# Inverse roots of mean squares: one GpSimd power in place of an integer guess and Newton steps on VectorE

## The chip, the cores and the metric

The kernel runs on one core of a Trainium2 chip. The metric is the device time of one execution, in microseconds (us); the median of three runs is given. In the profile the engines are PE (TensorE's matmuls), PEld (its weight loads), DVE (VectorE), ACT (ScalarE), POOL (GpSimd) and SP (the queue that issues most transfers).

## The reference, cut to what matters

A denoising step of two layers over 17 tiles of 128 tokens (2048 latent tokens and a prompt of 128), width 1024. Layer 0 mixes gated linear attention (GLA) and an S5 state space model, layer 1 windowed attention and a short convolution. In four places rows are normalised by their root mean square:

```python
def rmsnorm(x, w):
    xf = x.astype(jnp.float32)
    y = xf * lax.rsqrt(jnp.mean(xf * xf, axis=-1, keepdims=True) + EPS) * w
    return y.astype(x.dtype)

h = rmsnorm(x, norm_w) * (1.0 + scale) + shift       # input of layer 0, input of layer 1: 1024 wide
o = rmsnorm(o, gla_onorm)                            # output of a GLA head: 128 wide
q, k = rmsnorm(q, q_norm_w), rmsnorm(k, k_norm_w)    # 8 query heads and 2 key heads: 64 wide
```

## The kernel before, in words

Each engine works through its own list of instructions in order, and semaphores tie the lists together. The program is written tile by tile; a scheduler then fixes the order of each list when the program is built, from its own estimates. So a change in one helper can move instructions that it does not touch.

The work runs in five stages. **Phase 1** (`phase1`, to about 275 us) walks the 17 tiles: the square sums of a tile's rows (L275, ACT), the inverse root (L276, for two tiles at a time), the scaling of the rows (L278, DVE), eight transposes on PE and the modulation on ACT (L236, L240), the split into a high and a low float32r part (L242, L244, DVE), and 24 products for each of three outputs (L337, L338, PE). The log-gates of two tiles follow (`gates`, L876 to L884). Beside it the scheduler puts the S5 parameters on DVE (`s5_setup`, L401 to L458); when these are ready, POOL computes the first S5 tables (L571 to L573, L655 to L657). The second stage is the **S5 core** with the first dense passes. The third, from about 700 us, holds the other dense passes, the backward GLA states and the modulation rows of layer 1. **Phase 4** (`phase4`, about 940 to 1390 us) takes one GLA chunk after another: POOL prepares decay arguments in eight steps (`gla_arg`, L976 to L979), ACT and DVE finish them (L980, L981), PE multiplies keys by queries (L1054), DVE merges the products (L1061), PE sums the values (L1069 to L1071), and then the chunk's rows are copied (L1073), squared (L1078), and scaled by the inverse root (L1079) on POOL (L1080). One chunk later the rows are transposed (L1152), and yet one later comes the out-projection (L100 to L102) with the residual (L1124), the square sum (L1166), the inverse root (L1168), the scaling (L1169) and the transposes (L236) for layer 1. The **layer 1** passes follow: queries, keys and gate (`qkv_pass`, about 1390 to 1640 us, with the inverse roots of ten heads a tile at L1234, their use at L1237 and L1238, rotary products on POOL at L1257 and transposes at L1269 and L1275), the convolution, and attention with the last projection (from 2015 us).

The helper that the diff touches is `rsqrt` (L83 to L95). It has four callers: L276 with 128x2 values (eight times, and once 128x1 for the last tile), L1079 with 128x4, L1168 with 128x1 and L1234 with 128x10 (17 times each): 60 calls.

Of the kernel before, what the change touches and what calls it, by code (L numbers as in the profile page):

```python
# [36 lines left out]
class Ring:  # L37
    """Slots taken in turn; each has a pool of its own, and is waited for by itself."""
# [10 lines left out]
class Kernel:  # L49
# [12 lines left out]
    def bank(self, tag, shape=(128, 512), dt=F32):  # L62
        """A PSUM bank: D dense products, T transposes, W the rest."""
        pool, bufs = (self.wp, 4) if tag == "W" else (self.pp, 2)
        return pool.tile(list(shape), dt, name="ps" + tag, tag=tag, bufs=bufs)

    def pair(self, shape):
        """Two PSUM banks, the first dimension over them."""
# [14 lines left out]
    def rsqrt(self, pool, tag, ss, shape, n):  # L83
        """1/sqrt(ss/n + eps) on VectorE."""
# [3 lines left out]
        t = pool.tile(shape, F32, name="rst", tag=tag + "t")  # L88
        nc.vector.tensor_scalar(v, ss, 1.0 / n, EPS, op0=OP.mult, op1=OP.add)
        nc.vector.tensor_scalar(y.bitcast(I32), v.bitcast(I32), -0.5, 1597463007.0, op0=OP.mult, op1=OP.add)  # L90
        for _ in range(3):
            nc.vector.scalar_tensor_tensor(t, y, -0.5, y, op0=OP.mult, op1=OP.mult)
            nc.vector.tensor_tensor(t, t, v, op=OP.mult)
            nc.vector.scalar_tensor_tensor(y, t, 1.5, y, op0=OP.add, op1=OP.mult)
        return y  # L95

    def mm3(self, out, lh, ll, rh, rl, start, stop):
        """out += (lh+ll)^T (rh+rl) without the product of the two low parts."""
        mm = self.nc.tensor.matmul
        mm(out, lh, rh, start=start, stop=False)  # L100
        mm(out, lh, rl, start=False, stop=False)  # L101
        mm(out, ll, rh, start=False, stop=stop)  # L102

    # ------------------------------------------------------------------ set-up
    def setup(self, es):
        nc, a = self.nc, self.a
        c = self.const = self.pool(es, "const", 1, side="left")
        self.ident = self.load(c, "ident", a["ident"])
        self.nw = self.load(c, "nw", a["nw"])
        cc = self.load(c, "cc", a["cc"])  # L110
        t = c.tile([128, 8, 2], F32, name="silt")
        # silu of the conditions, hi and lo
# [7 lines left out]
        # per layer: scale' = (1 + scale) norm_w and shift, feature-major; gate rows on all partitions  # L120
# [24 lines left out]
    def ada(self, l, j, wp, ring=None, room=None, bufs=4):  # L145
        """Columns 512 j.. of layer l's modulation rows: shift, scale' or the gate's rows."""
# [3 lines left out]
    def ada_cols(self, l, c0, n, wp, ring, room, bufs):  # L150
# [5 lines left out]
        # products of the rows' high parts, and of their low parts below  # L156
# [32 lines left out]
    def split_w(self, dst_h, dst_l, src, cols, stp, tag, ks):  # L189
        """dst_h/dst_l [128, 8, cols] of f32r from weight rows [1024, cols] in DRAM."""  # L190
# [7 lines left out]
    def ring(self, es, name, n, side):  # L198
        """Slots of 256 weight columns, hi and lo of f32r."""
        return Ring(*[self.pool(es, f"{name}{j}", 1, side=side) for j in range(n)])  # L200

    def slot(self, ring, src, nk=8, tag="w"):
        """256 weight columns [128 nk, 256] of DRAM -> [128, 2 (hi, lo), nk, 256] of f32r."""
# [12 lines left out]
    def stage(self, shape):  # L216
        """[128, ..] of the staging buffers."""
# [4 lines left out]
    def split(self, dst, src):  # L222
        """dst [128, 2 (hi, lo), ..] of f32r from src."""
# [3 lines left out]
    def make_h(self, l, s, xs, wk, hp=None):  # L227
        """h^T of one token tile from its normalised rows, [128, 8, 128]; with hp also its hi and lo of f32r."""
# [18 lines left out]
    # ------------------------------------------------------------------ phase 1  # L247
# [3 lines left out]
    def phase1(self, e5):  # L251
        nc, a = self.nc, self.a
        with ExitStack() as es:
# [34 lines left out]
            def tail(i):  # L288
                pl = self.bank("T", (96, 128))
                nc.tensor.transpose(pl, low.pop(i).rearrange("p z c -> p (z c)"), self.ident)  # L290
                # tile 0, then two tiles at a time
# [4 lines left out]
                # hi, hi, lo  # L296
# [6 lines left out]
            with ExitStack() as es2:  # L303
# [7 lines left out]
                # v | lf | lb, and u  # L311
                for k in range(8):
                    for c0, n, src in ((0, 544, 512), (544, 512, 1568)):
                        self.split_w(wh[:, :, c0 : c0 + n], wl[:, :, c0 : c0 + n], a["w_in_e"][:, src : src + n], n, ap, "w1st", (k,))
                    if k == 3:
# [4 lines left out]
                        # hi, lo, hi  # L320
# [38 lines left out]
    # ------------------------------------------------------------------ S5 parameters  # L359
    def s5_setup(self, es):  # L360
# [23 lines left out]
        with ExitStack() as e2:  # L384
# [27 lines left out]
            def exp(x):  # L412
                """e^x to float32's accuracy."""
# [13 lines left out]
                # below -87 the result is under float32's normal range: 0  # L427
# [9 lines left out]
            # th = k pi/2 + r  # L437
# [33 lines left out]
            # c = (lb - 1) / lam  # L471
# [15 lines left out]
            # [bb_re; bb_im] and [bb_im; bb_re]  # L487
# [10 lines left out]
            def powers(P, Q, hi):  # L498
                """P + iQ at 1 given: the powers up to hi, by doubling."""
# [22 lines left out]
            # e^{16 i theta}  # L522
# [6 lines left out]
            def unit(P, Q, u, v):  # L529
                """P + iQ back to modulus 1."""  # L530
# [18 lines left out]
    # ------------------------------------------------------------------ S5 core  # L549
    def s5_core(self, es):  # L550
# [7 lines left out]
        def weights(g):  # L558
            """C lambda^tau of a group; the kernel's rows when a quad's are there."""
# [40 lines left out]
        def tables(g0):  # L600
            """cos and [sin; -sin] of the chunk phases of two groups: [128, g, d, 138]."""
# [27 lines left out]
        def first(g):  # L629
            """Loads, phase tables, and lambda^tau bb for the chunks' end states."""  # L630
# [28 lines left out]
        def second(g):  # L659
            """The chunks' end states and the scan over chunks."""  # L660
# [9 lines left out]
            # the increments' weights, transposed: [128 (s, h), d, half, 128 (re|im)]  # L670
# [33 lines left out]
        def third(g):  # L704
            """Outputs (step, h) x chunk: latent chunks, one unused column, prompt chunks."""
# [33 lines left out]
    # ------------------------------------------------------------------ dense passes over h^T  # L739
    def fm_pass(self, hp, blocks, use, hd=None, tag="D", lag=0, parts=None):  # L740
        """Feature-major products: for pieces of 272 tokens and blocks of 128 columns, use(blk, piece, psum)."""
# [37 lines left out]
    def col_slots(self, ring, src, c0, n):  # L779
        """n columns from c0 as slots, and their blocks of 128."""  # L780
# [9 lines left out]
    def qz_pass(self, hp, blocks):  # L790
        """Queries and keys (four blocks) and the S5 gate (four blocks), feature-major."""
# [8 lines left out]
    def zg_pass(self, hp, blocks):  # L800
        """2 silu(z_gla), feature-major."""
# [10 lines left out]
    def glu_pass(self, p):  # L812
        """The S5 branch's gated linear unit and gate: ys_d."""
# [8 lines left out]
        # z of 128 features: [(g, h), step from the chunk's end, chunk]  # L822
# [949 lines left out]
```

## Time and profile before

| what | us |
|---|---|
| three runs | 2440.71, 2440.75, 2435.2 (median 2440.71) |
| span of the profiled execution, first to last instruction | 2431.9 |
| PE busy in that span | 2296.6 (94%) |
| DVE busy | 1770.2 (73%) |
| ACT, POOL busy | 1035.7 and 889.1 |

The page gives the profiled execution by its span and lists no time of its own beside it; the span is 3.3 us under the lowest run and 8.8 us (0.36%) under the median. An engine's busy time counts overlapping instructions once. [...]

### The profile page before, as it was taken

Reading aid. Unit: us, or ns where it says so; the run is one execution under the profiler, and the core shown is the slowest. Engines: PE = TensorE matmul, PEld = TensorE weight load, DVE = VectorE, ACT = ScalarE, POOL = GpSimd, SP = SyncE. Lnnn points to the kernel's source line nnn. Section 1 sums busy time; section 2 is a strip of 40 time slices with the busy share of each in tenths; the row PEclk is TensorE's granted clock in tenths of the full one; section 3 lists DMA queues with packets and bytes.
Section 4 is the critical chain, followed back from the end, with each engine's and each line's share of the span. In section 5 each row is a group of like instructions: output and inputs, shape, how many; then the busy total and the mean of one; then the engine's idle time right before and its main releaser. Section 6 shows DMA issues by size and latency. Waiting matters only on the chain.

```text
span 2431.9 us, 47923 instructions
## 1 busy us (share of the span) xinstructions
PE 2296.6 (94%) x17657; PEld 2118.7 (87%) x17657; DVE 1770.2 (73%) x4033; ACT 1035.7 (43%) x2462; POOL 889.1 (37%) x1351
## 2 busy tenths in 40 slices
PE   7998898899999997999999999999999998999998
PEld 4887787787788776888888999999999998999998
DVE  7998699999976887888888675556334336666765
ACT  7453532222244665455454432234112115565653
POOL 4117047777612525767675021111101102222221
PEclk8999999999999998899999999999999998999999
DMA  8442562233269776333333552235215213222221
GB/s 302 139 149 83 164 166 78 82 85 90 82 177 305 228 241 193 96 116 124 113 122 107 176 162 79 79 110 171 68 55 140 63 54 120 88 87 88 88 70 57
DMA packets 321906, 303.96 MB, mean 125 GB/s; under 512 B 44208, under 2 KB 281408, under 8 KB 321672
## 3 DMA queue, kind: packets, MB, share of 16 engines
q1 hardware_dynamic: 263672, 227.70, 31.3%
q10 hardware_dynamic: 48112, 42.38, 5.4%
q0 software_dynamic: 9888, 30.83, 3.4%
q8 instruction: 139, 2.28, 0.4%
q14 instruction: 95, 0.78, 0.1%
HBM read 212.43 MB, written 88.39 MB: 124 GB/s over the span
## 4 chain that ended last, share of the span: by engine, by line
PE 56%; DVE 6%; DMA 4%; issue 3%; ACT 2%; POOL 2%; SPq 0%; ACTq 0%; DVEq 0%; POOLq 0%
PE psW L102 7%; PE psW L100 7%; PE psW L101 7%; PE psD L100 7%; PE psD L102 6%; PE psD L101 6%; PE psP L1054 3%; PE psW L1483 2%; PE psW L1436 2%; PE psT L1471 2%; DMA wst<-in_w_ada_dram 1%; PE psP L1069 1%; PE psP L1071 1%; DMA zr<-z_d 1%; PE psT L928 1%
## 5 line engine op out<-in xcount | busy, mean ns | idle before, releaser
L100 PE MATMUL psD<-slot,yT 128*128 128x256 f32 x1088 | 316.3, 291 | 1.5 <-ACT yT L1098 1.3
L102 PE MATMUL psD<-slot,yT 128*128 128x256 f32 x1088 | 312.7, 290 | 0.0
L101 PE MATMUL psD<-slot,yT 128*128 128x256 f32 x1088 | 309.0, 285 | 0.0
L102 PE MATMUL psW<-hq,slot 128*128 128x272 f32 x1024 | 293.4, 288 | 0.0
L101 PE MATMUL psW<-hq,slot 128*128 128x272 f32 x1024 | 291.8, 286 | 0.0
L100 PE MATMUL psW<-hq,slot 128*128 128x272 f32 x1024 | 288.7, 287 | 0.0
L101 PE MATMUL psD<-hq,slot 128*128 128x272 f32 x768 | 225.6, 294 | 17.4 <-DVE hq L225 17.4
L100 PE MATMUL psD<-hq,slot 128*128 128x272 f32 x768 | 227.1, 298 | 11.0 <-ACT fo L787 10.5
L102 PE MATMUL psD<-hq,slot 128*128 128x272 f32 x768 | 225.3, 294 | 0.0
L100 PEld LDWEIGHTS psD<-slot,yT 128*128 128x128 f32 x1088 | 207.1, 190 | 9.0 <-ACT yT L1098 1.9
L101 PEld LDWEIGHTS psD<-slot,yT 128*128 128x128 f32 x1088 | 206.9, 190 | 2.2 <-issue 0.2
L102 PEld LDWEIGHTS psD<-slot,yT 128*128 128x128 f32 x1088 | 204.9, 190 | 4.4 <-issue 1.9
L102 PEld LDWEIGHTS psW<-hq,slot 128*128 128x128 f32 x1024 | 192.7, 188 | 0.0
L101 PEld LDWEIGHTS psW<-hq,slot 128*128 128x128 f32 x1024 | 192.1, 188 | 0.0
L100 PEld LDWEIGHTS psW<-hq,slot 128*128 128x128 f32 x1024 | 191.3, 189 | 0.0
L213 DVE TENSOR_TENSOR slot<-wst,slot 128x512 fp32r<-128x512 f32 x176 | 122.2, 705 | 65.7 <-ACT slot L212 65.1
L101 PEld LDWEIGHTS psD<-hq,slot 128*128 128x128 f32 x768 | 145.7, 190 | 25.7 <-DVE hq L225 21.0
L100 PEld LDWEIGHTS psD<-hq,slot 128*128 128x128 f32 x768 | 145.3, 190 | 19.1 <-ACT fo L787 12.9
L212 ACT CAST slot<-wst 128x512 fp32r<-128x512 f32 x176 | 106.6, 621 | 118.1 <-DMA wst<-in_w_in_o_dram 31.9
L1445 DVE CUSTOM_DVE_ANT_0 sc<-psW,amask,sink 128x512 f32<-128x512 f32 (+1 forms) x128 | 93.7, 732 | 83.5 <-PE psT L1471 76.5
L102 PEld LDWEIGHTS psD<-hq,slot 128*128 128x128 f32 x768 | 145.5, 190 | 7.9 <-issue 7.8
L980 ACT ACTIVATE arg<-arg 128x512 f32<-128x512 f32 x119 | 75.0, 630 | 141.5 <-POOL arg L979 132.1
(387 smaller groups left out, 6794.0 us busy)
## 6 DMA issues: line engine op xcount, KB each, us to landing
wst<-h_d SPq DMA_DIRECT2D x136, 272.0 KB
wst<-in_w_ada_dram SPq DMA_DIRECT2D x64, 256.0 KB
h_d<-hf SPq DMA_DIRECT2D x17, 512.0 KB
x_d<-x ACTq DMA_DIRECT2D x17, 512.0 KB
h_d<-hf ACTq DMA_DIRECT2D x17, 512.0 KB
wst<-h_d SPq DMA_DIRECT2D x34, 256.0 KB
qf<-qa_d SPq DMA_DIRECT2D x34, 256.0 KB
hq<-x_d SPq DMA_DIRECT2D x17, 512.0 KB
```

Source lines behind the costliest of these rows:

```text
L100: mm(out, lh, rh, start=start, stop=False)
L101: mm(out, lh, rl, start=False, stop=False)
L102: mm(out, ll, rh, start=False, stop=stop)
L212: nc.scalar.copy(r32(w[:, 0, k : k + 2]), st)
L213: nc.vector.tensor_tensor(r32(w[:, 1, k : k + 2]), st, w[:, 0, k : k + 2], op=OP.subtract)
L928: nc.tensor.matmul(kv[o : o + 64, pr, :], kt[:, pr, o : o + 64], v[:, h * 128 : h * 128 + 128], start=True, stop=True, tile_position=(0, o),)
L980: nc.scalar.activation(arg, arg, AF.Exp, scale=0.0625)
L1054: nc.tensor.matmul(pv[:, hh, pr, :], ak[o : o + 64, pr, :], aq[o : o + 64, pr, :], start=True, stop=True)
L1436: nc.tensor.matmul(out, r32(qs[:, j, h]), kk, start=j == 0, stop=j == 1)
L1445: V.tensor_tensor_reduce(sv, ps, mask, 1.0, sk[:, h : h + 1], op0=OP.add, op1=OP.max, accum_out=m)
L1471: nc.tensor.transpose(pt[:, c, :], t[:, 128 * c : 128 * c + 128], self.ident)
L1483: nc.tensor.matmul(po[kv][:, j % 2], r32(VV[:, b, kv]), r32(t[:, x, :, c, :]), start=c + x == 0, stop=c + x == nb)
```

## The change

`rsqrt` keeps the first step on DVE, v = ss/n + eps. The integer guess and the nine Newton operations on DVE go; one GpSimd `tensor_tensor` raises v to a column of -0.5 that is written once in `setup`. The rest of the diff takes out comments and docstrings, so line numbers after the helper are two lower.

```diff
     def rsqrt(self, pool, tag, ss, shape, n):
         nc = self.nc
         v = pool.tile(shape, F32, name="rsv", tag=tag + "v")
         y = pool.tile(shape, F32, name="rsy", tag=tag + "y")
-        t = pool.tile(shape, F32, name="rst", tag=tag + "t")
         nc.vector.tensor_scalar(v, ss, 1.0 / n, EPS, op0=OP.mult, op1=OP.add)
-        nc.vector.tensor_scalar(y.bitcast(I32), v.bitcast(I32), -0.5, 1597463007.0, op0=OP.mult, op1=OP.add)
-        for _ in range(3):
-            nc.vector.scalar_tensor_tensor(t, y, -0.5, y, op0=OP.mult, op1=OP.mult)
-            nc.vector.tensor_tensor(t, t, v, op=OP.mult)
-            nc.vector.scalar_tensor_tensor(y, t, 1.5, y, op0=OP.add, op1=OP.mult)
+        e = self.mhalf if len(shape) == 2 else self.mhalf.unsqueeze(2)
+        nc.gpsimd.tensor_tensor(y, v, e.to_broadcast(shape), op=OP.pow)
         return y
...
         self.ident = self.load(c, "ident", a["ident"])
+        self.mhalf = c.tile([128, 1], F32, name="mhalf")
+        nc.gpsimd.memset(self.mhalf, -0.5)
```

The scheduler's new order shows at three places. First, DVE in phase 1, at the last tile's inverse root (s5A and wu are tables of the S5 parameters; now two lines lower). Before:

```order
L89 TENSOR_SCALAR rsv<-ss_124 128x1
L278 TENSOR_SCALAR xt<-xt,rsy 128x1024 x2
L405 TENSOR_TENSOR s5A_1970<-s5A_1970,wu_2256 128x576
L405 TENSOR_TENSOR s5A_1971<-s5A_1971,wu_2256 128x576
L343 COPY vo<-psW 128x272
L90 TENSOR_SCALAR rsy<-rsv 128x1
L299 TENSOR_TENSOR lr<-psT,lr 32x128
```

Now:

```order
L403 TENSOR_TENSOR s5A_1902<-s5A_1902,wu_2188 128x576
L403 TENSOR_TENSOR s5A_1903<-s5A_1903,wu_2188 128x576
L240 CAST ht<-hf 128x512
L242 TENSOR_TENSOR ht<-hf,ht 128x1024
L88 TENSOR_SCALAR rsv<-ss_126 128x1
L341 COPY vo<-psW 128x272
L297 TENSOR_TENSOR lr<-psT,lr 32x128
L240 CAST ht<-hf 128x512
L874 TENSOR_TENSOR gm<-b_124,psW 128x512 x2
L276 TENSOR_SCALAR xt<-xt,rsy 128x1024
```

The last tile's inverse root now comes after the S5 tables, and five other instructions stand between its first step (now L88) and the scaling that uses it (now L276).

Second, POOL at the same time: the first S5 tables (ct and e; L571 to L573 and L655 to L657 before, two lower now) with the last tile's power among them. Now:

```order
L882 DMA b_d<-ge 128x4x256
L569 TENSOR_TENSOR ct_2742<-s5M,s5CY 128x272
L570 TENSOR_TENSOR ct<-s5R,s5CX 128x272
L569 TENSOR_TENSOR ct_2747<-s5M,s5CY 128x272
L570 TENSOR_TENSOR ct<-s5R,s5CX 128x272 x9
L654 TENSOR_TENSOR e<-s5R,s5X 128x256 x2
L570 TENSOR_TENSOR ct<-s5R,s5CX 128x272
L571 TENSOR_TENSOR ct<-ct,ct_2742 128x272
L570 TENSOR_TENSOR ct<-s5R,s5CX 128x272
L90 TENSOR_TENSOR rsy<-rsv,mhalf 128x1
L571 TENSOR_TENSOR ct<-ct,ct_2747 128x272
```

The power (L90) stands behind 17 of these tables in POOL's list; before, POOL had no part in an inverse root.

Third, POOL in a chunk of phase 4, where q is the last decay argument of a chunk. Now:

```order
L966 TENSOR_TENSOR q<-qk 128x256
L90 TENSOR_TENSOR rsy<-rsv,mhalf 128x1
L974 TENSOR_TENSOR arg<-B 128x2x64
L975 TENSOR_TENSOR arg<-B 128x2x64
L976 TENSOR_TENSOR arg<-B 128x2x64
L977 TENSOR_TENSOR arg<-B 128x2x64
L90 TENSOR_TENSOR rsy<-rsv,mhalf 128x4
L974 TENSOR_TENSOR arg<-B 128x4x32
L1078 TENSOR_TENSOR gy<-gy,rsy 128x512
```

Each chunk has gained the two powers here, and the scaling of the rows (gy, L1080 before) has moved up among the decay arguments, from behind the third group to the middle of the second.

## Rows read from the trace of the kernel before

**Rows 1.** The page: span, and busy time of each engine.

```profile
span 2431.9 us, 47923 instructions
PE 2296.6 (94%) x17657; PEld 2118.7 (87%) x17657; DVE 1770.2 (73%) x4033; ACT 1035.7 (43%) x2462; POOL 889.1 (37%) x1351
```

**Rows 2.** Windows: stretch, length, busy per engine (instructions), PE clock, DMA share, GB/s.

```profile
60.00:180.00 120.00, 116.38 (x748) 105.24 (x746) 115.94 (x382) 62.86 (x136) 15.76 (x30) 1.00 0.45 146
...
220.00:240.00 20.00, 13.15 (x65) 10.84 (x64) 16.20 (x16) 7.21 (x14) 9.58 (x13) 0.83 0.17 60
...
970.00:980.00 10.00, 6.19 (x34) 5.16 (x34) 9.57 (x19) 3.13 (x5) 10.00 (x19) 0.50 0.18 52
...
1050.00:1200.00 150.00, 148.97 (x1229) 129.41 (x1228) 129.71 (x307) 76.68 (x190) 107.33 (x195) 1.00 0.38 120
...
1500.00:1635.00 135.00, 135.00 (x1131) 135.00 (x1130) 73.93 (x190) 32.88 (x76) 25.21 (x45) 1.00 0.30 88
```

**Rows 3.** Groups by line: two of four removed DVE operations; busy us, mean ns, idle.

```profile
L93 DVE TENSOR_TENSOR rst<-rst,rsv 128x1 f32<-128x1 f32 (+3 forms) x180 | 39.7, 221 | 3.8
...
L90 DVE TENSOR_SCALAR rsy<-rsv 128x1 int32<-128x1 int32 (+3 forms) x60 | 11.1, 185 | 0.8
```

**Rows 4.** Timeline of DVE: start, us, instruction; a chain of nine by itself (first, last).

```profile
61.68 0.16 DVE L92 SCALAR_TENSOR_TENSOR rst<-rsy 128x2 f32<-128x2 f32 x1
...
63.25 0.16 DVE L94 SCALAR_TENSOR_TENSOR rsy<-rst,rsy 128x2 f32<-128x2 f32 x1
```

**Rows 5.** Timeline of DVE: a removed operation between others.

```profile
21.92 0.15 DVE L93 TENSOR_TENSOR rst<-rst,rsv 128x2 f32<-128x2 f32 x1
21.99 0.69 DVE L167 TENSOR_TENSOR w1l<-wada,w1l 128x512 fp32r<-128x512 f32 x1
```

**Rows 6.** Timeline of DVE: the last tile's chain of nine (first, last), beside POOL's tables.

```profile
184.76 0.60 DVE L92 SCALAR_TENSOR_TENSOR rst<-rsy 128x1 f32<-128x1 f32 x1
...
189.66 0.57 DVE L94 SCALAR_TENSOR_TENSOR rsy<-rst,rsy 128x1 f32<-128x1 f32 x1
```

**Rows 7.** Timeline of PE, 60 to 240 us: five of eight waits, with what ended each.

```profile
100.68 0.73 PE L338 MATMUL psD<-w1h,ht 128*128 128x512 f32 x2 [1.70 <-DVE ht L244]
...
180.10 0.73 PE L338 MATMUL psD<-w1h,ht 128*128 128x512 f32 x2 [1.08 <-DVE ht L244]
...
196.66 0.52 PE L337 MATMUL psW<-w1h,ht 128*128 128x272 f32 x2 [2.76 <-DVE ht L244]
...
225.27 0.39 PE L337 MATMUL psW<-w1h,ht 128*128 128x272 f32 x1 [3.69 <-DVE gm L876]
...
236.03 0.66 PE L236 MATMUL psT<-ident,xt 128*128 128x128 f32 x4 [1.71 <-DVE lr L299]
```

**Rows 8.** Timeline of DVE: a conversion beside POOL's tables.

```profile
210.29 14.21 DVE L242 CAST ht<-hf 128x512 fp32r<-128x512 f32 x1 [1.10 <-ACT hf L240]
```

**Rows 9.** Timeline of PE at the start of phase 4: first and last of three waits.

```profile
971.91 1.23 PE L1054 MATMUL psP<-arg 64*128 64x128 f32 x8 [0.65 <-DVE rsy L94]
...
978.40 0.79 PE L1069 MATMUL psP<-sf,hq 64*128 64x128 f32 x2 [2.21 <-DVE hq L1061]
```

**Rows 10.** Lines of POOL: a small copy and a small product (min/median/max ns).

```profile
L1311 POOL COPY crow<-crow x28: 184/184/246, 1638.2 to 1984.3; 128x2 f32<-128x2 f32 x28
...
L1257 POOL TENSOR_TENSOR au<-an,ropes x64: 516/528/1017, 1409.0 to 1616.4; 128x160 f32<-128x160 f32 x64
```

**Rows 11.** Groups by line: POOL's longest computing instruction.

```profile
L1422 POOL TENSOR_TENSOR qs<-qf,qs 128x1024 fp32r<-128x1024 f32 x17 | 40.6, 2391 | 101.6 <-DVE pT L225 60.5 <-ACT qs L1421 41.1
```

**Rows 12.** Timeline of POOL: first of the S5 tables, and one near their end.

```profile
183.29 0.65 POOL L571 TENSOR_TENSOR ct<-s5M,s5CY 128x272 f32<-128x272 f32 x1 [4.32 <-DVE s5A L405]
...
222.97 1.24 POOL L571 TENSOR_TENSOR ct<-s5M,s5CY 128x272 f32<-128x272 f32 x2
```

**Rows 13.** Timelines of DVE and PE in the query pass: a tile's rows ready, their transposes.

```profile
1460.80 0.28 DVE L1266 TENSOR_TENSOR ao<-an,au 128x128 f32<-128x128 f32 x1
...
1465.42 0.60 PE L1269 MATMUL psT<-ident,ao 128*128 128x128 f32 x4
```

## The prediction

> **What bounds the kernel now.** I read the page first: PE is busy for 2296.6 of 2431.9 us [rows 1], so at most 135 us of the span can be won by anything that makes PE wait less, and an engine with spare time can lose work without the end moving. The windows say where those 135 us are [rows 2]. From 1050 us on, through phase 4 and the query pass, PE is busy for 148.97 of 150 and 135.00 of 135 us at a granted clock of 1.00: there the matmuls are the bound, DVE has a seventh to nearly half of its time free, and a faster inverse root moves nothing. In phase 1 the picture differs: from 60 to 180 us DVE is busy for 115.94 of 120 us and PE for 116.38, so the two run head to head. The timeline of PE then gives the reasons of its stops: eight waits between 60 and 240 us [rows 7], every one ended by DVE. Three of them, from 100.68 to 180.10, come to 3.7 us; five, from 196.66 to 236.03, to 9.6 us. At the start of phase 4 there are three more, from 971.91 to 978.40, of 3.8 us together, the first of which names the Newton steps [rows 9]. These 17 us are what the change can reach. The S5 core holds no inverse root, and PE's list is word for word the same there in both programs.
>
> **What is removed.** 60 calls lose ten DVE operations each: the guess 60 times and three kinds of Newton operation 180 times each, 600 in all, at a mean of 185 to 221 ns [rows 3], so about 120 us of busy time. What DVE gains is less: an operation between others takes 0.07 us until the next one starts [rows 5], while a chain by itself costs about 0.2 for each, 1.73 us for nine [rows 4] and 1.9 with the guess. Over the first seven calls of phase 1 that follow 45 us that is 70 operations, between 5 and 14 us. The last call is dearer: its nine operations run from 184.76 to 190.23, 5.5 us, while POOL computes [rows 6]. So DVE gets back between 10 and 19 us of the first 190; I take 15, ten of them before the last call. Of the other 51 calls, 34 lie in phase 4 and 17 in the query pass, where PE covers them; if PE were faster there, they would be worth 51 times up to 1.9 us.
>
> **What is added.** 60 powers on POOL, and a memset that nothing waits for. The trace has no power. From below its price is that of POOL's smallest two-column copy, 0.184 us; from above, with nothing better, POOL's longest computing instruction, 2.39 us for 128x1024 [rows 10, 11]. I take 0.5 us, near the 0.528 of a product with a broadcast operand over 160 columns [rows 10], which is the nearest shape in kind; both ends stay in the range. At 0.5 us an inverse root lasts less than the 1.73 us chain even with two hand-overs between engines, which I put at 0.2 us each from the spacing of dependent DVE operations in the same chain. At 2.39 it lasts about a microsecond longer, but DVE is free meanwhile, except where the scaling stands right behind v, as in the second to fourth call.
>
> [...]
>
> **What is moved: phase 1 (minus 6.5 us).** With 15 us less on DVE, the split parts of a tile (L242, L244) come earlier, and the three waits of 3.7 us before the tables go. The wait of 2.76 at 196.66 follows directly on the dear chain and should go as well. That is 6.5 us. The four later waits, 6.9 us, have another cause: a conversion took 14.21 us from 210.29 [rows 8], to the end of a row of POOL tables that runs from 183.29 to about 224.2 [rows 12]. The tables stay, so I leave these 6.9 us and the lowered clock there (0.83 from 220 to 240) as they are. New is a wait: the last tile's power stands behind 17 tables on POOL, about 12 us at some 0.7 each, and DVE's scaling of that tile's rows waits for it, with the next split parts queued behind. Because the S5 parameters are finished 5 to 14 us sooner, by the DVE time won before them, DVE has that much in hand, so I charge nothing; without that cover it costs up to 5 us.
>
> [...]
>
> **Phase 4's start (minus 1.2 us).** From 965 to 979 us the second chunk has no other matmuls beside it, PE runs at a clock of 0.50, and DVE and POOL are both full (9.57 and 10.00 of 10 us from 970 to 980) [rows 2]. DVE loses ten operations there, 0.7 to 1.9 us by the bounds above, and PE's waits of 3.8 us [rows 9] are what that could shorten. But POOL gets a power, and the scaling of the rows moves up before decay arguments that used to come first. I take minus 1.2, between minus 3.8 and plus 3. Later in phase 4 and in the query pass: nothing, covered by PE. In the query pass a tile's rows are ready at 1461.1 and transposed at 1465.42 [rows 13], 4.3 us of slack on top of the 1.9 us chain that goes.
>
> Sum: 6.5 + 1.2 = 7.7 us off the profiled span of 2431.9, that is 2424.2. The median of the runs stands 8.8 above that span; with the same distance, 2433.0.
>
> **The rivals.**
> - *Hidden anyway.* The scheduler's new list puts other S5 steps where the Newton steps were, so the split parts come no earlier and PE keeps its waits; phase 4's start gives and takes. For it: DVE is full either way from 60 to 180 us. Against: S5 work is finite, and 15 us less must show. The time is 2437 to 2444.
> - *The blocked conversion goes too.* The tables then meet other DVE work, so the 6.9 us vanish, with up to 3 us of clock, and all of phase 4's 3.8: 3.7 + 2.8 + 6.9 + 3 + 3.8, about 20 off, 2420.
> - *A longer block.* The tables start up to 14 us sooner and hold another conversion for some 14 us as in [rows 8], or DVE stands for the last tile's power. PE has split parts in hand, so it loses some 8 to 14 us, with up to 3 at phase 4's start; the 6.5 won before go against it: 2442 to 2451.
> - *A slow power makes the query pass wait (slower).* If the power is evaluated column by column in software, ten columns cost far more than 0.5 us. The point from which it decides is 4.3 + 1.9 = 6.2 us for a 128x10 power: beyond it the transposes of every tile come late on PE's list. At 10 us each of 17 tiles loses 3.8, some 65 us: about 2500. Against: POOL's longest row is 2.39 us for 1024 columns. For: nothing in the trace bounds a power.
>
> **How the numbers follow.** About 0.3% (7 us) is what a measurement of this kernel can tell from no change, so the line runs at 2433.4. The forecast (4 to 13 us off) has 0.50, two thirds of it beyond the line; hidden 0.22; the conversion gone too 0.12; a longer block 0.08, of which 0.05 is slower; a slow power 0.08. Faster: 0.34 + 0.12 = 0.46. Same: 0.16 + 0.22 + 0.03 = 0.41. Slower: 0.13. The range leaves out the slow power and a few hundredths at each end: 2420 to 2450.
>
> **What would show it.** Right: no PE wait ended by L244 between 60 and 200 us, DVE busy about 15 us less up to 190, a POOL row for L90 of about half a microsecond, phase 4 and the query pass as long as before. Wrong: a L90 row of several microseconds; a DVE wait at the last tile's scaling that names POOL's power and is followed by a PE wait; PE gaps in the query pass before the transposes; or phase 1 as long as before with DVE less full.

## The result, and the profile after

The changed kernel takes **2452.07 us** (median of 4 runs, 2449.5 to 2452.27); the kernel before, run beside it, 2439.45 (4 runs, 2435.2 to 2440.75). The ratio is 1.0055, 95% interval 1.0039 to 1.0070: slower by 12.6 us, 2 us above the upper end of the predicted range. The profiled execution is one of 2452.01 us; that of before was one of 2435.2 us, 4 us under its median.

The page of the changed kernel, span and busy times [rows 1]:

```profile
span 2450.2 us, 47334 instructions
PE 2302.0 (94%) x17657; PEld 2124.8 (87%) x17657; DVE 1669.6 (68%) x3433; ACT 1037.3 (42%) x2462; POOL 942.3 (38%) x1412
```

DVE did lose 100.6 us of work. PE is no less busy, but the span is 18.3 us longer. The windows (busy of PE, PEld, DVE, ACT, POOL, then PE's clock) tell where [rows 2]:

```profile
60.00:180.00 120.00, 116.66 (x752) 105.56 (x751) 111.20 (x321) 60.65 (x129) 18.96 (x34) 1.00 0.42 136
200.00:220.00 20.00, 14.44 (x77) 12.54 (x77) 16.18 (x13) 8.84 (x20) 12.49 (x18) 0.83 0.24 79
220.00:240.00 20.00, 8.97 (x39) 7.64 (x40) 13.91 (x8) 1.96 (x7) 9.42 (x16) 0.66 0.08 27
...
1050.00:1200.00 150.00, 149.90 (x1248) 130.38 (x1246) 107.16 (x186) 77.34 (x190) 107.78 (x199) 1.00 0.39 120
1500.00:1635.00 135.00, 135.00 (x1133) 135.00 (x1132) 59.87 (x100) 30.01 (x71) 44.51 (x54) 1.00 0.27 82
```

Phase 4 and the query pass are full, as before. Between 200 and 240 us PE stands for 16.6 of 40 us. The granted clock falls in each of the two long stops: in slices of 5 us it is 0.62 and 0.69 from 200 to 210 us (in slices of 1 us, 0.50 from 202 to 208), 1.00 from 210 to 220, then 0.67, and 0.50 from 225 to 235. PE's timeline gives the waits of phase 1 [rows 7]:

```profile
48.31 1.12 PE L234 MATMUL psT<-ident,xt 128*128 128x128 f32 x4 [3.85 <-ACT hf L238]
...
104.68 0.74 PE L336 MATMUL psD<-w1h,ht 128*128 128x512 f32 x2 [1.54 <-DVE ht L242]
...
120.15 0.52 PE L335 MATMUL psW<-w1h,ht 128*128 128x272 f32 x2 [1.65 <-DVE ht L242]
...
203.88 0.82 PE L335 MATMUL psW<-w1h,ht 128*128 128x272 f32 x2 [6.18 <-DVE ht L242]
...
231.03 1.22 PE L336 MATMUL psD<-w1h,ht 128*128 128x512 f32 x2 [11.49 <-DVE ht L242]
```

DVE at the same place (idle time before an instruction in brackets), beside the conversion of [rows 8]:

```profile
189.07 1.28 DVE L874 TENSOR_TENSOR gm<-b,psW 128x512 f32<-128x512 f32 x2 [2.91 <-PE psW L873]
194.00 7.09 DVE L276 TENSOR_SCALAR xt<-xt,rsy 128x1024 f32<-128x1024 f32 x1 [3.65 <-POOL rsy L90]
...
202.15 0.41 DVE L240 CAST ht<-hf 128x512 fp32r<-128x512 f32 x1
202.60 1.23 DVE L242 TENSOR_TENSOR ht<-hf,ht 128x1024 fp32r<-128x1024 f32 x1
...
210.85 0.43 DVE L240 CAST ht<-hf 128x512 fp32r<-128x512 f32 x1
213.11 16.60 DVE L240 CAST ht<-hf 128x512 fp32r<-128x512 f32 x1 [1.83 <-ACT hf L238]
```

and POOL, whose power stands where the order showed it, behind 17 tables:

```profile
181.71 0.75 POOL L569 TENSOR_TENSOR ct<-s5M,s5CY 128x272 f32<-128x272 f32 x1 [0.66 <-DVE s5A L403]
...
193.40 0.57 POOL L90 TENSOR_TENSOR rsy<-rsv,mhalf 128x1 f32<-128x1 f32 x1
193.95 0.77 POOL L571 TENSOR_TENSOR ct<-ct,ct 128x272 f32<-128x272 f32 x1
...
199.91 0.64 POOL L569 TENSOR_TENSOR ct<-s5M,s5CY 128x272 f32<-128x272 f32 x1
206.03 1.04 POOL L345 COPY l<-vo 128x96 f32<-128x96 f32 x1 [5.49 <-ACT vo L342]
```

Two words for what follows. DVE **stands** when it is idle for a result, here 3.65 us for the last tile's power. It is **held** when its own row is long while POOL computes: the scaling, 0.75 us in the median of its calls, lasts 7.09, until just after POOL's run of tables ends at 200.55 (199.91 + 0.64), and a conversion of 0.43 lasts 16.60.

The table gives, for the same PE instruction in two traces, how much later it starts than in the profile of before (from the traces of the experiments below too; e13 is the kernel before with a tile that nothing reads, so it serves as a second profile of before):

| start in before, us | after | e13 | e1 | e2 | e3 | e5 | e9 | e14 |
|---|---|---|---|---|---|---|---|---|
| 45.30, first L337, first product of phase 1 | +5.2 | -0.6 | +0.6 | +5.0 | +4.4 | +4.7 | +5.6 | +4.4 |
| 282.69, last L337, end of phase 1 | +13.9 | -0.8 | +0.4 | +13.3 | -0.4 | +2.8 | +2.5 | -8.4 |
| 940.34, first L1054 of phase 4 | +14.9 | +4.2 | +4.2 | +20.2 | +3.2 | +6.3 | +4.0 | -3.4 |
| 1342.99, last L1054 | +16.3 | +0.7 | -0.2 | +23.7 | +3.7 | +8.2 | +6.4 | -2.0 |
| 1654.70, first L1363, after the query pass | +16.5 | +1.1 | +0.6 | +23.8 | +3.0 | +6.9 | +5.0 | -2.5 |
| 2427.26, last product | +18.3 | +0.7 | +2.4 | +27.3 | +2.4 | +8.9 | +5.1 | -0.6 |

So of the 18.3 us between the two profiles 13.9 exist when phase 1 ends. Later rows differ by up to 4.2 us even between before and e13, so a difference of that size in one profile is not read as an effect. Where an expectation below gives the start of the first product (56 us, or 60 to 61), it counts from a point 10.6 us earlier than the profile does: that is the row at 45.30 here.

### The profile page after: what moved, and what is told of

Same layout as the page of the kernel before. It is cut to its first block, busy times and chain, and to the rows that moved or that the text cites. A ratio compares the mean times of both kernels' runs of the same rounds, so it can differ in the third digit from the quotient of the medians.

```text
span 2450.2 us, 47334 instructions
## 1 busy us (share of the span) xinstructions
PE 2302.0 (94%) x17657; PEld 2124.8 (87%) x17657; DVE 1669.6 (68%) x3433; ACT 1037.3 (42%) x2462; POOL 942.3 (38%) x1412
## 4 chain that ended last, share of the span: by engine, by line
PE 55%; DVE 4%; issue 4%; DMA 4%; POOL 3%; ACT 2%; SPq 0%; ACTq 0%; DVEq 0%; POOLq 0%
PE psW L96 7%; PE psW L97 7%; PE psW L98 7%; PE psD L96 6%; PE psD L97 6%; PE psD L98 6%; PE psW L1481 2%; PE psW L1434 2%; PE psP L1052 2%; PE psT L1469 2%; PE psP L1067 1%; PE psP L1069 1%; DMA zr<-z_d 1%; POOL arg L974 1%; POOL arg L976 1%
## 5 line engine op out<-in xcount | busy, mean ns | idle before, releaser
L90 POOL TENSOR_TENSOR rsy<-rsv,mhalf 128x1 f32<-128x1 f32 (+3 forms) x60 | 72.4, 1207 | 309.1 <-DVE rsv L88 278.7
```

What stands on the lines that cost most here:

```text
L90: nc.gpsimd.tensor_tensor(y, v, e.to_broadcast(shape), op=OP.pow)
```

## The experiments

Line numbers of the variants are shifted by a few; the tiles' names tell which line it is. Times are medians, ratios are against the kernel before, run beside each. Theory A: the loss is made in phase 1. Theory B: the power itself is dear, wherever something waits for it.

**e1 and e2: the two halves of the change.** Newton kept in phase 1 (e1, the test as shown), or everywhere else (e2, with the test turned round).

```diff
+        if tag == "rs0":
+            nc.vector.tensor_scalar(y.bitcast(I32), v.bitcast(I32), -0.5, 1597463007.0, op0=OP.mult, op1=OP.add)
+            for _ in range(3):
...
+            return y
         nc.gpsimd.tensor_tensor(y, v, e.to_broadcast(shape), op=OP.pow)
```

> The three-step Newton form stays in phase 1 (its 9 calls); the other 51 roots go to the power. Every engine's order in phase 1 is then the one of the kernel before, and from phase 4 on about the changed kernel's. Theory A (the loss is made in phase 1: first products 4 to 5 us late, the block of S5 tables some 9 us longer): the time comes back to 2437 to 2442 us, the first product of phase 1 starts near 56 us and the DVE waits of PE in 180 to 260 us are again near 10 us. Theory B (the power itself costs, 1.07 us in the median where 0.5 was taken, on every call that something waits for, most of all the 128x10 calls of phase 4 and of the query pass): the time stays at 2448 to 2452 us.

> The reverse: the power in phase 1 only, Newton in phase 4 and the query pass. Every engine's order in phase 1 is the changed kernel's. Theory A: 2449 to 2454 us, first product near 61 us, two DVE waits of PE of about 6 and 11 us between 200 and 245 us. Theory B: 2437 to 2442 us.

e1: 2439.66 us, ratio 1.0003 (0.9992 to 1.0014). e2: 2459.02, 1.0074 (1.0055 to 1.0093). Theory B falls: 51 powers from phase 4 on cost nothing that shows, and nine in phase 1 bring the whole loss. e2 is even above the changed kernel; the table puts the difference after phase 1, where e2 has Newton and the changed kernel the power. As e1 and before do not differ there, I do not read a gain of the power from it; why the two parts do not add is open.

**e3: one call.** Newton for the last tile alone; the diff is against e1.

```diff
-        if tag == "rs0":
+        if tag == "rs0" and shape[1] == 1:
```

> The changed kernel with Newton for the last tile's row (128x1) alone, ten instructions on DVE at the place of the POOL power that stood behind 17 S5 tables; all else keeps its order but for a handful of rows. Theory A1 (in the block it is DVE's standing for that power, 3.65 us, and then the scaling held 7.09 us): PE's DVE waits in 180 to 260 us fall from 19 us to about 10 us and the time to 2441 to 2445 us. Theory A2 (the block is long because the S5 tables run packed together on POOL and hold whatever DVE runs, with or without this power): the waits stay at 15 us or more and the time at 2449 to 2453 us.

2439.84, ratio 0.9999 (0.9989 to 1.0010). One of 60 calls carries all of the loss, more than either theory of the expectation gave it. PE's DVE waits from 180 to 260 us fall from 18.9 to 4.4 us. The scaling is there at once, and the hold of a conversion is back in the form of [rows 8]:

```profile
187.62 0.79 DVE L284 TENSOR_SCALAR xt<-xt,rsy 128x1024 f32<-128x1024 f32 x1
...
212.96 12.25 DVE L248 CAST ht<-hf 128x512 fp32r<-128x512 f32 x1 [1.11 <-ACT hf L246]
```

The first product is still 4.4 us late, and by the end of phase 1 that is gone: the late start is absorbed in the block.

**e4: the late start.** In the changed kernel ScalarE squares tiles 2 and 3, after waiting 2.99 us for their load, before it scales tile 0; in the kernel before it scaled tile 0 first (at 42.50). After:

```profile
44.39 1.06 ACT L273 ACTIVATE sqj<-xt 128x1024 bf16<-128x1024 f32 x1 [2.99 <-DMA xt<-in_xs_dram]
...
46.77 2.88 ACT L238 ACTIVATE hf<-psT,msh,msc 128x128 f32<-128x128 f32 x8
```

```diff
...
-                    nc.scalar.activation(junk, xt[j], AF.Square, accum_out=ss[:, j : j + 1])
+                    with self.tc.issue_after(self.hf_first.ins) if i == 2 else ExitStack():
+                        nc.scalar.activation(junk, xt[j], AF.Square, accum_out=ss[:, j : j + 1])
```

> The changed kernel with ScalarE's squares of tiles 2 and 3 ordered behind tile 0's first eight scale-and-shift instructions, as they stood in the kernel before; the order of some other rows of phase 1 moves with it. If the 4 to 5 us at the first product come from ScalarE standing for the load of tiles 2 and 3 ahead of that work: first product back at 56 to 57 us, and 3 to 5 us less in all (2447 to 2449 us) if nothing else moves. If it comes from late weights or from the w1l subtractions on POOL: the first product stays at 60 to 61 us.

The first product is back (1.0 us late), and the median is 2447.32, ratio 1.0039 (1.0024 to 1.0055). So the cause of the late start is shown. What it is worth is not: the profiled run was one of 2455.35 us, and its block is the changed kernel's (a scaling of 7.70, a conversion of 16.60 us).

**e5: the last row called earlier.** It changes place with tiles 14 and 15, whose power now falls into the block.

```diff
-                if i % 2 and i + 1 < NTILE:
+                if i % 2 and i + 1 < NTILE - 1:
                     rows(i + 1)
...
                 if i == 10:
+                    rows(16)
                     self.s5_setup(e5)
```

> The changed kernel with the last tile's load, square, power and scaling called ahead of the S5 set-up, so that its power is issued on POOL before the tables (all else moves by a few rows; no Newton anywhere). Theory A1 (the loss is DVE standing at the last tile's scaling, for a power that is queued behind 17 tables, and then held in it while the tables run on): no scaling is left inside the block, one hold of 12 to 14 us at a conversion stays as before, PE's DVE waits in 180 to 260 us fall to about 10 us, and the time to 2437 to 2442 us. Rival (Newton's ten small instructions helped in another way, by breaking up the POOL tables while they ran beside them): the time stays above 2446 us, since no such instructions are here either.

2442.24, ratio 1.0013 (1.0003 to 1.0023). The rival falls, but the edit did less than meant: DVE stands 3.87 us for the other power, and then two scalings pass unheld:

```profile
194.71 1.78 DVE L276 TENSOR_SCALAR xt<-xt,rsy 128x1024 f32<-128x1024 f32 x2 [3.87 <-POOL rsy L90]
...
216.34 10.78 DVE L240 CAST ht<-hf 128x512 fp32r<-128x512 f32 x1 [1.11 <-ACT hf L238]
```

**e6, e7, e8: the form of the held instruction.** The last tile's scaling (e6), the conversions of tiles 11 to 16 as well (e7), and the same in the kernel before (e8), as operations of two tensors.

```diff
-                    nc.vector.tensor_scalar(xt[j], xt[j], rs[:, n : n + 1], None, op0=OP.mult)
+                    if j >= 16:
+                        nc.vector.tensor_tensor(xt[j], xt[j], rs[:, n : n + 1].to_broadcast([128, 1024]), op=OP.mult)
...
-                nc.vector.tensor_copy(r32(h[:, 0, kk * 4 : kk * 4 + 4]), f[:, kk * 4 : kk * 4 + 4])
+                d, g = r32(h[:, 0, kk * 4 : kk * 4 + 4]), f[:, kk * 4 : kk * 4 + 4]
+                if two:
+                    nc.vector.tensor_tensor(d, g, g, op=OP.max)
...
```

> The changed kernel with the last tile's scaling written as a product of two tensors (the row's factor read for each element) in place of a one-tensor instruction; the power stays behind the tables and DVE still stands for it. Tells the stand (3.65 us) from the hold (7.09 us) inside theory A1. If the hold is of one-tensor instructions with both ends in SBUF alone: the scaling takes 1.2 to 2.5 us and 5 to 6 us come back in the block, though the time falls by as much only if the next hold doesn't take the place (2444 to 2448 us). If any instruction is held at that place: 7 us again and 2450 to 2453 us.

> As the run before, and the conversions of tiles 11 to 16 as well written as an operation of two tensors (the maximum of the tile with itself, rounded on output). If only one-tensor instructions with both ends in SBUF are held while POOL runs tables: no DVE instruction over 3 us in 180 to 245 us, PE's DVE waits there fall from 19 us to under 8 us, and the time to 2434 to 2441 us. If the hold is not of that form: a 10 to 17 us instruction stays there, and 2448 to 2453 us.

> The same edit to the kernel before (Newton everywhere): the 14.21 us hold at the conversion was worth about 10 us of PE waiting at most, less what the start of the following tiles gives back. If the hold goes with the form: 2430 to 2436 us, no DVE instruction over 3 us in 180 to 245 us. If not: 2437 to 2441 us.

e6: 2447.58, ratio 1.0038 (1.0023 to 1.0053). e7: 2454.49, 1.0067 (1.0046 to 1.0088). e8: 2447.67, 1.0033 (1.0020 to 1.0047). My idea of the form was wrong. The scaling of e6 passes in 1.79 us, but the same instruction of e7 at the same place is held, and so are two-tensor conversions and the low part:

```profile
193.70 1.79 DVE L277 TENSOR_TENSOR xt<-xt,rsy 128x1024 f32<-128x1024 f32 x1 [3.57 <-POOL rsy L90]
```

```profile
192.91 7.62 DVE L281 TENSOR_TENSOR xt<-xt,rsy 128x1024 f32<-128x1024 f32 x1 [3.93 <-POOL rsy L90]
...
211.23 9.03 DVE L242 TENSOR_TENSOR ht<-hf 128x512 fp32r<-128x512 f32 x1 [0.24 <-ACT hf L238]
220.30 10.13 DVE L246 TENSOR_TENSOR ht<-hf,ht 128x1024 fp32r<-128x1024 f32 x1
```

In e8 one conversion is held 19.09 us, the second half of its tile, with no scaling held before it:

```profile
203.84 0.87 DVE L244 TENSOR_TENSOR ht<-hf 128x512 fp32r<-128x512 f32 x1
204.96 19.09 DVE L244 TENSOR_TENSOR ht<-hf 128x512 fp32r<-128x512 f32 x1 [0.25 <-ACT hf L240]
```

```profile
225.36 1.22 PE L345 MATMUL psD<-w1h,ht 128*128 128x512 f32 x2 [14.22 <-DVE ht L248]
```

e6 tells less than hoped: its block costs only 2.2 us at the end of phase 1, and it loses 9.4 more before phase 4 begins, in rows that I cannot tie to the edit (e13 loses 4.9 there too).

**e9: the queue place alone.** The power stays; the tables stand behind it.

```diff
...
+                with self.tc.issue_after(self.pow16.ins) if g < 8 else ExitStack():
                     G.tensor_tensor(t1, pw(M), cv(self.s5_CY), op=OP.mult)
                     G.tensor_tensor(ct[:, d], pw(R), cv(self.s5_CX), op=OP.mult)
```

> The changed kernel with the S5 tables ordered on POOL behind the last tile's power in place of 17 of them ahead of it: the power, DVE's work and every other order stay as they are but for four rows. If the loss is the stand of DVE for a power in that queue place, with what it brings on (the hold of the scaling, and the long conversion hold falling one tile earlier): no DVE wait for the last tile's power over 1.5 us, the scaling under 2.5 us, PE's DVE waits in 180 to 260 us 5 to 11 us, and the time 2436 to 2442 us. If the power form itself, or the earlier tables, make the block longer: 2448 us or more.

2438.30, ratio 0.9997 (0.9986 to 1.0009): the loss is gone with every power in place. POOL's power, then the scaling on DVE and the later conversion:

```profile
183.30 0.57 POOL L90 TENSOR_TENSOR rsy<-rsv,mhalf 128x1 f32<-128x1 f32 x1 [2.38 <-DVE rsv L88]
```

```profile
183.91 1.14 DVE L276 TENSOR_SCALAR xt<-xt,rsy 128x1024 f32<-128x1024 f32 x1 [0.76 <-POOL rsy L90]
...
212.79 15.27 DVE L240 CAST ht<-hf 128x512 fp32r<-128x512 f32 x1 [1.11 <-ACT hf L238]
```

**e10: the wait without a power.** e3, with Newton's result passed through a POOL copy.

```diff
...
+            z = pool.tile(shape, F32, name="rsz", tag=tag + "z")
+            nc.gpsimd.tensor_copy(z, y)
+            return z
```

> The reverse, without a power at that place: the last tile's root by Newton on DVE as in the run with Newton for the last tile (2439.8 us), but its result passed to the scaling through a POOL copy of 128x1, which stands behind some 20 tables. If it is the wait for POOL's queue, not the power, that costs: DVE stands several us for the copy, the scaling may be held as well, and the time is 2446 to 2456 us. If the power's own time counted: 2438 to 2442 us, as without the copy.

2440.04, ratio 1.0008 (0.9998 to 1.0018). The time lies in the second range, but not for its reason, which e9 excludes: the power is in place there and costs nothing. The copy does stand behind the tables and DVE does stand for it, 2.77 us; only the hold did not follow:

```profile
196.88 1.12 DVE L286 TENSOR_SCALAR xt<-xt,rsz 128x1024 f32<-128x1024 f32 x1 [2.77 <-POOL rsz L97]
```

```profile
196.80 1.71 POOL L580 TENSOR_TENSOR ct<-s5R,s5CX 128x272 f32<-128x272 f32 x2
```

So a stand of 2.8 us by itself is not what costs. With e5 that leaves the hold, which may follow a stand or not. Here DVE came to the scaling while POOL was in a product (196.80); in the changed kernel it came in an addition of two tables (193.95). No run reproduces the hold behind a stand without a power.

**e11 and e12: operands in PSUM.** ScalarE leaves the scaled tile in its bank for tiles 11 to 16, DVE reads it there, and ScalarE copies it out afterwards; in the kernel before (e11) and in e9 (e12).

```diff
-                nc.scalar.activation(f[:, k, :], pt[:, j, :], AF.Identity, bias=sh, scale=sc)
...
+                nc.scalar.activation(pt[:, j, :] if ps else f[:, k, :], pt[:, j, :], AF.Identity, bias=sh, scale=sc)
...
+                nc.vector.tensor_copy(r32(h[:, 0, kq]), pt)
+                nc.vector.tensor_tensor(r32(h[:, 1, kq]), pt, h[:, 0, kq], op=OP.subtract)
+                nc.scalar.copy(f[:, kq], pt)
```

> The kernel before, with ScalarE leaving the scaled tile in its PSUM bank for tiles 11 to 16 (and copying it to SBUF after that), and DVE's conversion and low part reading the bank. In every block so far an instruction with an operand in PSUM passed (0.29 to 0.69 us) while one with all operands in SBUF was held 7 to 19 us. If that is the rule: no DVE instruction over 3 us at the conversions in 180 to 245 us, PE's DVE waits there under 6 us, and 4 to 8 us gained in phase 1 (2431 to 2436 us) unless the banks, kept longer, hold the transposes. If the operand's place does not matter: a hold of over 9 us remains and 2438 to 2444 us.

> Both edits on the changed kernel: tables behind the last tile's power, and conversions of tiles 11 to 16 from PSUM. If both theories hold: no stand for the power, no hold at a conversion, and 2428 to 2435 us; if only the first: 2436 to 2442 us.

In both, every conversion and low part takes 0.69 us amid the tables; in e11 nothing is held, and phase 1 ends 7.1 us earlier than before. In e12 an instruction with all operands in SBUF takes the hold instead:

```profile
214.74 0.69 DVE L243 CAST ht<-psT 128x512 fp32r<-128x512 f32 x1 [2.86 <-ACT psT L240]
```

```profile
216.78 8.41 DVE L883 SCALAR_TENSOR_TENSOR ge<-gm 128x1024 f32<-128x1024 f32 x1
```

The times do not follow: e11 2440.49, ratio 1.0009 (1.0000 to 1.0018), e12 2444.15, 1.0023 (1.0010 to 1.0036). The profile of e11 has 4.8 us left at phase 4's start and 1.1 at the last L1054. What the expectation of e11 says of the operand's place holds in all of these rows (0.69 us with an operand in PSUM, 8.41 us for the held instruction with all operands in SBUF); that it is worth time does not show.

**e13, e14, e15: the pace, and all three losses together.** In a long run of products from the first L1363 to the first L1436 (1655 to 2013 us in the kernel before) PE waits for nothing in the kernels compared here (it is busy for 300.00 of 300 us in the windows below), and its order is the same in all of them, but those with the new constant tile are slower from product to product. e13 adds only the tile to the kernel before (first two lines); e14 is e9 with 64 bytes for it (last two); e15 is e14 with the edit of e4.

```diff
+        self.mhalf = c.tile([128, 1], F32, name="mhalf")
+        nc.gpsimd.memset(self.mhalf, -0.5)
...
-        self.mhalf = c.tile([128, 1], F32, name="mhalf")
+        self.mhalf = c.tile([128, 16], F32, name="mhalf")[:, 0:1]
```

> [...] In the run of products from the first L1363 to the first L1436 the kernel before and its variants without the tile take 124.4 ns from one product to the next (358.5 us), and every kernel with the tile 125.3 to 125.4 ns (361.1 to 361.3 us), at the same clock of 1.00 and in the same order. Theory P (the tiles' place in SBUF): 125.3 ns and 361.1 us here too, 2 to 3 us of the time. Theory Q (something that the power leaves behind on POOL or in its schedule): 124.4 ns and 358.5 us, and no difference in the time.

> The kernel with the tables behind the last tile's power (2438.3 us), with the constant tile 64 bytes wide in place of 4, so that the tiles after it lie at the same place modulo 64 bytes as in the kernel before; all orders as they were. Theory P with a step of 64 bytes: 124.4 ns and 358.5 us in that run of products, and 2435 to 2437 us. If it is not the place modulo 64: 125.3 ns still, 2437 to 2440 us.

> The run before, and ScalarE's squares of tiles 2 and 3 behind tile 0's first eight scale-and-shift instructions: the three losses found (late squares, the wait in the block, the pace) taken away at once. If they add up: first product at 56 to 57 us, the DVE waits of PE in 180 to 260 us under 11 us, and 2431 to 2436 us, under the kernel before. If the late start is absorbed by the block anyway (as it was where the last tile kept Newton): the same as the run before, 2435 to 2438 us.

The same window of 300 us (PE's first number in brackets counts its products), of the kernel before, of the changed one, of e13 and of e14:

```profile
1700.00:2000.00 300.00, 300.00 (x2413) 300.00 (x2412) 121.86 (x248) 60.15 (x113) 33.63 (x82) 1.00 0.26 76
```

```profile
1700.00:2000.00 300.00, 300.00 (x2395) 300.00 (x2395) 122.98 (x252) 61.50 (x121) 33.76 (x83) 1.00 0.28 81
```

```profile
1700.00:2000.00 300.00, 300.00 (x2396) 300.00 (x2395) 119.43 (x241) 59.94 (x112) 33.76 (x82) 1.00 0.26 76
```

```profile
1700.00:2000.00 300.00, 300.00 (x2407) 300.00 (x2406) 119.97 (x246) 58.60 (x110) 33.50 (x82) 1.00 0.26 76
```

The tile that nothing reads brings the slower pace (361.3 us for the stretch where before took 358.5), so it does not come from the power. The 64-byte tile, in the order of e9 and with nothing changed but the width of that tile, gives two thirds back (359.4 where e9 took 361.1). So the pace changed with that tile and its width; that it is the place of the tiles after it is my theory, and was not shown, since no trace gives a tile's place. But e13 takes 2438.24 us, ratio 0.9991 (0.9980 to 1.0002): the 2.8 us do not reach the total, and are no part of the loss that I can claim.

e14: 2434.73, ratio 0.9985 (0.9973 to 0.9996), the only one of the fifteen whose interval lies wholly under 1, and by so little that among fifteen it may be chance; I do not claim a gain. The conversion that e9 had for 15.27 us, in the same order on every engine, is not held in its profile:

```profile
210.79 0.72 DVE L240 CAST ht<-hf 128x512 fp32r<-128x512 f32 x1 [1.11 <-ACT hf L238]
```

e15: 2440.09, ratio 0.9999 (0.9991 to 1.0008). The first product is 1.2 us late instead of 4.4, the conversion is held again for 15.24 us, and the lower time of e14 is gone. The losses do not add up: of the 9.1 us by which the profiles of e15 and e14 end apart, 6.6 exist when phase 1 ends.

## Why the prediction was wrong

**The step that failed** is the sentence on the last tile's power: "so I charge nothing; without that cover it costs up to 5 us". Both halves failed. The cover was to be S5 parameters 5 to 14 us sooner; POOL's first table starts at 181.71 against 183.29 [rows 12], 1.6 us sooner, although DVE's busy time up to 180 us fell by 12.4 us (the 15 that I took for the first 190 was near). Nor would an earlier table help: in e4, without the late start, it comes at 178.10, 5.2 us sooner than before, and DVE still stands 2.84 us for the power and the scaling is held 7.70. And the price was put at a stand, while the dear thing is what a stand lets in. Before, the last tile's Newton chain kept DVE going from 184.76 to 190.23 [rows 6], and the scaling followed at once. Now DVE arrives at the scaling from a pause, 0.05 us after POOL has begun its next table, an addition (194.00 and 193.95), and is held until the tables stop; a PE wait follows. That is what the prediction listed as a sign of being wrong. That this one place in POOL's queue makes the loss is shown by e3 and e9, which differ from the changed kernel in little else; that a stand alone does not, by e5 and e10.

**Why 7 us of hold cost more than 7.** In the kernel before, the long conversion came when the tile in front of it had both its parts (its low part, L244, from 206.18; the hold from 210.29), and PE had a whole tile's products to run meanwhile. In the changed kernel the hold of the scaling delays the second half of a tile's conversion to 202.15, and the next hold, at 213.11, falls on a second half instead of a first one. PE then has nothing, and its longest wait in the block is 11.49 us instead of 3.69 [rows 7]. Before:

```profile
206.18 1.56 DVE L244 TENSOR_TENSOR ht<-hf,ht 128x1024 fp32r<-128x1024 f32 x1
```

This reading comes from the two orders, and the other traces bear it out. In the five profiles where a long hold falls on a tile's second half (the changed kernel, e2, e4, e7, e8) PE's DVE waits from 180 to 260 us come to 17.9 to 20.5 us, and phase 1 ends 8.6 to 13.9 us later than before. In the nine where it falls on a first half (before, e1, e3, e5, e6, e9, e10, e13, e15) they come to 4.4 to 10.7 us, and phase 1 ends at most 2.8 us later. e8 says most: no scaling is held in it (1.64 us), only a conversion, and it loses 8.6 us. No run moved a hold from one half to the other and changed nothing else.

**Point by point.**
- *The rival "a longer block"* gave 2442 to 2451 us, for earlier tables that hold another conversion for some 14 us, or for a stand at the last tile's power. It was the nearest, with too small a chance (0.08) and about a microsecond too small a price: the stand came, and it brought a hold of the scaling that the rival did not name.
- *Minus 6.5 us in phase 1*: three DVE waits before the tables came to 3.7 us, and three still come to 3.3 (1.54 at 104.68, 1.65 at 120.15, 0.15 at 146.16); DVE is still busy for 19.72, 19.87 and 19.64 of 20 us from 80 to 140 us. The wait of 2.76 at 196.66, which was to go, became 6.18 at 203.88. Not foreseen at all: ScalarE's order changed too, and the first product comes 5.2 us late. I had followed the order on DVE and POOL only.
- *The power's price*: 0.5 us was taken. The medians are 0.55 for 128x1, 0.71 for 128x2, 1.39 for 128x4 (the row below, 1.01, is its fastest) and 1.98 for 128x10, and 1.07 over all 60; the longest is 2.33, so all lie within the bounds of 0.184 and 2.39. The 0.70 us of a 128x2 power (the first row below) are over four times the 0.16 us of one removed operation [rows 4]. Being off by half cost nothing, as e1 shows.

```profile
54.66 0.70 POOL L90 TENSOR_TENSOR rsy<-rsv,mhalf 128x2 f32<-128x2 f32 x1 [0.17 <-DVE rsv L88]
...
1009.99 1.01 POOL L90 TENSOR_TENSOR rsy<-rsv,mhalf 128x4 f32<-128x4 f32 x1 [0.22 <-DVE rsv L88]
...
1466.41 1.99 POOL L90 TENSOR_TENSOR rsy<-rsv,mhalf 128x10 f32<-128x10 f32 x1 [3.60 <-DVE rsv L88]
```

- *Phase 4 and the query pass*: nothing lost that shows, as said (e1). DVE stands 26.1 us in the query pass for powers of 128x10, and PE is busy for 135.00 of 135 us there. The slow power did not come: 1.99 us is far from the 6.2 from which it would decide.
- *The blocked conversion goes too*: not in the changed kernel; it does in e14, and phase 1 is then 8.4 us shorter, of which 0.6 are left at the last product.

## What to carry to other kernels

When a step moves to another engine's queue, look at what that queue holds at the moment of each call, and put the new instruction ahead of a run of others: here one call of 60, 0.57 us of work behind 17 tables, cost 12.6 us, and ordering the tables behind it took the loss away. Price the wait by what the waiting engine then meets, not by its length: here stands of 2.8 to 3.9 us left 0.7 to 2.8 us at the end of phase 1 where the scaling was not held (e5, e6, e10), and 10.8 to 13.9 us where it was (the changed kernel, e2, e4, e7). And compare the new order on every engine, those that the change doesn't touch included, since a program that a scheduler orders can move work on a third engine.

## What the runs showed of the hardware that I had not expected

- **DVE instructions were held for many POOL instructions.** The holds lasted 7.09 to 19.09 us, while POOL's tables took 0.6 to 0.8 us each. In the eight profiles whose rows of POOL reach to the end of the hold (before, the changed kernel, e2 to e5, e7, e8) it ended 0.3 to 1.1 us after POOL's last table ahead of a pause, but for one hold of e7, 9.03 us, that ended while POOL ran on.
- **Instructions with an operand in PSUM were not held.** Copies, products, conversions and low parts with an operand in PSUM took 0.29 to 0.69 us each in the block in the kernels quoted here (0.69 in e11 and e12), and every instruction held had all operands in SBUF, of one tensor or two. (Most instructions with all operands in SBUF were not held either.)
- **The order did not settle who was held.** e9 and e14 have the same order, and a conversion takes 15.27 us in one and 0.72 in the other; e6 and e7 have the same scaling at the same place, 1.79 and 7.62 us. One sign stands in the rows: the last tile's scaling as a one-tensor instruction was held in the three kernels where it started in an addition of two tables (the changed one, e2, e4), and passed in 0.79 to 1.14 us in the ten where it started in a product (before, e1, e3, e9 to e15). But e6's passed in an addition, and the conversion of [rows 8] was held in a product, so what decides it stayed open, and one profile of such a block is one throw.
- **PE's pace changed with a tile that nothing reads.** With a 4-byte constant that nothing reads (e13), 300 us of back-to-back products held 2396 instead of 2413, at the same order and a granted clock of 1.00 in both. The total did not show it.
